# Scores of a gated linear attention on quarters of the TensorE array: 32 keys per matmul with their own queries, collected in a compact tile

## The chip, the cores and the metric

The kernel runs on one core of a Trainium2 chip. Its time is the device time of one execution in microseconds (us), lower is better; of several runs the median is given. Engines are named as in the profile: PE is TensorE (PEld its weight loads), DVE is VectorE, ACT is ScalarE, POOL is GpSimd, SP is SyncE, which issues the transfers.

## The reference, cut to what matters

The reference is one decoder layer over 256 tokens: an RMSNorm, one wide input projection, three branches (gated linear attention, forgetting attention, cross-attention into 256 memory tokens), their gates, an output projection and a final RMSNorm. The change concerns the scores inside the gated linear attention. It has 4 heads with keys of 128 features and a decay for every feature and every token:

```python
b = jnp.cumsum(gi, axis=2)
...
diff = b[:, :, :, None, :] - b[:, :, None, :, :]
decay = jnp.exp(jnp.where(causal[None, None, :, :, None], diff, -jnp.inf))
scores = jnp.einsum('bhid,bhjd,bhijd->bhij', qi, ki, decay)
o_intra = jnp.einsum('bhij,bhje->bhie', scores, vi)
```

The score of query i and key j is a sum over 128 features of q, k and exp(b_i - b_j), with j not after i. All arithmetic is float32.

## The kernel before, in words

**The main work.** Nearly all of the time goes into projections of the normed tokens with float32 weights. Each weight piece of 1024 columns by 128 rows is loaded by SP (tile `raw`), rounded to a high part by ACT (`hi`, line 174) and subtracted to a low part by DVE (`lo`, line 187); PE multiplies with both. `natural` (lines 224 to 226) makes projections with the tokens on partitions, `transposed` (lines 254 and 259) those with the features on partitions. In `transposed` a group of four matmuls of 512 columns (L254) and four of 256 columns (L259) makes one step.

**The order of the work.** The order is written out by hand. Everything that isn't a projection is a Python generator in one of three lanes (`post`, `side`, `main`); after each step of a projection `pull()` advances each lane by one `yield`, and `yield n` leaves n - 1 pulls out. So small work is threaded between projection steps in program order, on each engine's own queue.

**The scores.** `gla_scores` (line 601) runs in the main lane. It treats 8 tiles (4 heads by 2 halves of 128 tokens), each with 128 keys and 128 queries, and a fixed ladder of levels: blocks of 32, of 8, of 2, and single tokens. At a level with blocks of s, the keys are referred to the end of their own block (`E`, lines 687 to 692), and the queries of later blocks inside the same stretch of 4s tokens are referred to the end of the first, second or third block of that stretch (`Q`, 96, 64 and 32 queries of each tile, 192 columns in all, lines 630 to 643). Both factors are exponentials that can't overflow.

For each tile the matmul of L718 multiplies all 128 keys with all 192 prepared queries, 128 partitions by 192 columns. Two tiles share a bank of PSUM, so a level has four groups of two matmuls, one group per pull. Of the 128x192 products only those in which the key's block belongs to the query's reference are wanted. DVE picks them with `copy_predicated` (L732) under a mask from POOL: three instructions per group, one for each part of Q, written into `gA`, the 8 tiles of 128x128 scores. The last level has a matmul with 64 odd queries and all 128 queries, and two instructions per group (masks `gpair` and `ident`). At the end `gla_out` uses `gA` as the weights of L748. A float32 matmul appears as two weight loads and two matmuls in the profile, so the 32 matmuls of L718 are 64 records of each kind.

**The same features elsewhere.** In the forgetting attention, L817 multiplies with 64 weight columns at a time: two heads write the upper and the lower half of one bank's partitions. It is the one place before the change where matmuls use a part of the array's columns.

Of the kernel before, what the change touches and what calls it, by code (L numbers as in the profile page):

```python
# [16 lines left out]
P = 128  # L17
# [34 lines left out]
N_WARM = 7  # L52

STEPS = (32, 8, 2)
Q_OFF = (0, 96, 160)
Q_N = 192
BR_KT = (range(0, 8), range(8, 12), range(12, 16))

# [2 lines left out]
def body(ctx, tc, xw, memT, xn, memn, wall, wsm, wup, cst, fgain, out):  # L61
# [425 lines left out]
        return r  # L487


    gmask = cpool.tile([P, len(STEPS), Q_N], F32, name="gmask")  # L490
    gpair = cpool.tile([P, 64], F32, name="gpair")
    dpool = ctx.enter_context(tc.tile_pool(name="dpool", bufs=1, space=bass.MemoryType.DRAM))
    drow = dpool.tile([1, 8 * S], F32, name="drow")

    def make_masks():

        nc.gpsimd.memset(gmask, 1.0)
        for li, s in enumerate(STEPS):
            for b in range(3):
                w, nb = (3 - b) * s, 32 // s  # L500
                mk_ = gmask[:, li, Q_OFF[b]:Q_OFF[b] + nb * w].rearrange("p (b s) -> p b s", s=w)
                nc.gpsimd.affine_select(out=mk_, in_=mk_, pattern=[[-4 * s, nb], [0, w]],
                                        compare_op=ALU.is_ge, fill=0.0, base=-b * s, channel_multiplier=1)
                nc.gpsimd.affine_select(out=mk_, in_=mk_, pattern=[[4 * s, nb], [0, w]],
                                        compare_op=ALU.is_ge, fill=0.0, base=(b + 1) * s - 1, channel_multiplier=-1)

        nc.gpsimd.affine_select(out=gpair, in_=ones[:, :64], pattern=[[-2, 64]], compare_op=ALU.is_equal,
                                fill=0.0, base=0, channel_multiplier=1)

    def scale_first():  # L510

# [89 lines left out]
    def gla_scores():  # L601
        gB, gq, gk = G["B"], G["q"], G["k"]
        gqf, gkf = gq.rearrange("p h s -> p (h s)"), gk.rearrange("p h s -> p (h s)")
        B4 = gB.rearrange("p (h t i) -> p h t i", h=4, t=2)

        def blocks(x, half, s):

            return x[:, 512 * half:512 * half + 512].rearrange("p (b s) -> p b s", s=s)

        def of_q(Q, b, s):  # L610
            w = (3 - b) * s
            return Q[:, :, Q_OFF[b]:Q_OFF[b] + 32 * (3 - b)].rearrange("p e (b s) -> p e b s", s=w)

        def later(x, half, b, s):

            v = blocks(x, half, 4 * s)[:, :, (b + 1) * s:]
            return v.rearrange("p (e b) s -> p e b s", e=4)

        def prep_keys(s):

            E = a4([P, 1024])
            Bv = gB.rearrange("p (b s) -> p b s", s=s)
            nc.vector.tensor_tensor(out=E.rearrange("p (b s) -> p b s", s=s),
                                    in0=Bv[:, :, s - 1:s].to_broadcast([P, 1024 // s, s]), in1=Bv,
                                    op=ALU.subtract)
            return E

        def prep_queries(s, half):

            Q = a4([P, 4, Q_N])  # L630
            for b in range(3):
                w, nb = (3 - b) * s, 32 // s
                end = blocks(gB, half, 4 * s)[:, :, (b + 1) * s - 1:(b + 1) * s]
                nc.vector.tensor_tensor(
                    out=of_q(Q, b, s), in0=later(gB, half, b, s),
                    in1=end.rearrange("p (e b) s -> p e b s", e=4).to_broadcast([P, 4, nb, w]),
                    op=ALU.subtract)
            return Q

        def times_q(Q, s, half):  # L640
            for b in range(3):
                nc.vector.tensor_tensor(out=of_q(Q, b, s), in0=of_q(Q, b, s),
                                        in1=later(gqf, half, b, s), op=ALU.mult)

        def pick(v, u):
            return v[:, :, u].rearrange("p (e b) -> p e b", e=4)

        def prep_pairs(half):

            Q = a4([P, 4, Q_N])  # L650
            Bh = blocks(gB, half, 2)
            nc.vector.tensor_tensor(out=Q[:, :, :64], in0=pick(Bh, 1), in1=pick(Bh, 0), op=ALU.subtract)
            nc.scalar.copy(Q[:, :, 64:], gqf[:, 512 * half:512 * half + 512].rearrange(
                "p (e i) -> p e i", e=4))
            return Q

        def times_odd(Q, half):
            nc.vector.tensor_tensor(out=Q[:, :, :64], in0=Q[:, :, :64],
                                    in1=pick(blocks(gqf, half, 2), 1), op=ALU.mult)
# [12 lines left out]
        nc.vector.tensor_tensor(out=cd[:, :, 0, :], in0=cd[:, :, 0, :], in1=gk[:, :, :P], op=ALU.mult)  # L672
        nc.vector.tensor_tensor(out=cd[:, :, 1, :], in0=cd[:, :, 1, :], in1=gq[:, :, P:], op=ALU.mult)
        yield 2
        ps = att()
        for h in range(4):
            MM(ps[:, h * P:(h + 1) * P], lhsT=cd[:, h, 0, :], rhs=cd[:, h, 1, :], start=True, stop=True)
        yield 1
        gX = G["X"] = a2([P, 4, P])
        nc.scalar.copy(gX, ps.rearrange("p (a b) -> p a b", a=4))  # L680
        yield from fox_decay()

        for li in range(len(STEPS) + 1):
            s = STEPS[li] if li < len(STEPS) else None
            Qs = []
            if s:
                E = prep_keys(s)
                yield 2
                nc.scalar.activation(E, E, AF.Exp, scale=1.0 / 16)
                Qs.append(prep_queries(s, 0))  # L690
                yield 2
                nc.vector.tensor_tensor(out=E, in0=E, in1=gkf, op=ALU.mult)
                nc.scalar.activation(Qs[0], Qs[0], AF.Exp, scale=1.0 / 16)
                yield 2
                Qs.append(prep_queries(s, 1))
# [5 lines left out]
                yield 2  # L701
            else:
                E = gkf
                for half in range(2):
                    Qs.append(prep_pairs(half))
                yield 2
                for half in range(2):
                    odd = Qs[half][:, :, :64]
                    nc.scalar.activation(odd, odd, AF.Exp, scale=1.0 / 16)
                yield 2  # L710
                for half in range(2):
                    times_odd(Qs[half], half)
                yield 2
            for c in range(4):
                ps = att()[:, :2 * Q_N].rearrange("p (a b) -> p a b", a=2)
                for j in range(2):
                    e = 2 * c + j
                    MM(ps[:, j, :], lhsT=E[:, e * P:(e + 1) * P], rhs=Qs[c // 2][:, e % 4, :],  # L718
                       start=True, stop=True)
                A2 = gA[:, 2 * c:2 * c + 2, :]  # L720
                if s:
                    places = [(A2.rearrange("p a (b s) -> p a b s", s=4 * s)[:, :, :, (b + 1) * s:],
                               gmask[:, li, Q_OFF[b]:Q_OFF[b] + 32 * (3 - b)].rearrange(
                                   "p (b s) -> p b s", s=(3 - b) * s),
                               ps[:, :, Q_OFF[b]:Q_OFF[b] + 32 * (3 - b)].rearrange(
                                   "p a (b s) -> p a b s", s=(3 - b) * s)) for b in range(3)]
                else:
                    places = [(A2.rearrange("p a (b s) -> p a b s", s=2)[:, :, :, 1], gpair, ps[:, :, :64]),
                              (A2, ident, ps[:, :, 64:])]
                yield 1  # L730
                for dst, mask, src in places:
                    nc.vector.copy_predicated(  # L732
                        dst, mask.bitcast(U32).unsqueeze(1).to_broadcast(list(src.shape)), src)
            yield 1

    def gla_out():
        oa = G["o"] = [a4([P, 1024]) for _ in range(NT)]
# [492 lines left out]
```

## Time and profile before

| | before |
|---|---|
| median of 3 runs | 810.05 us (809.97 to 810.63) |
| the profiled execution | 810.0 us |
| its span in the trace | 808.3 us |
| granted PE clock, mean | 0.997 |
| PE records of L718 | 64 loads, 64 matmuls, from 108.8 to 186.3 us |

The profile shows one execution. A group row reads: line, engine, operation, tiles written and read, shape, count, then busy time in us and mean ns of one, then the engine's idle time ahead of them. A row of the timeline reads: start in us, length, engine, line, operation, shape, count. PE's ends are modelled, so what a matmul costs is read from the starts of the rows around it, not from its length.

### The profile page before, as it was taken

To read this page: it belongs to the slowest core of one execution; us is meant where nothing else is said; L and a number is where in the kernel's file an instruction comes from. 1 tells how busy PE (TensorE), PEld (TensorE's weight loads), DVE (VectorE), ACT (ScalarE), POOL (GpSimd) and SP (SyncE) were. 2 spreads that over 40 slices of the span, in tenths; PEclk is the share of its full clock that TensorE was granted. 3 is DMA by queue.
4 is the path that set the end of the run, shared out by engine and by line. 5 is a ranking of instruction groups with operands and counts; after the bars stand their busy time and mean duration, and the time that the engine had idled before them with its cause. 6 is when DMAs were issued, how large, how long until landed. Compare 5 with 4: busy or idle time off the path is not lost.

```text
span 808.3 us, 9931 instructions
## 1 busy us (share of the span) xinstructions
PE 798.4 (99%) x3888; PEld 670.4 (83%) x3888; DVE 495.4 (61%) x697; ACT 403.9 (50%) x558; POOL 18.8 (2%) x36
## 2 busy tenths in 40 slices
PE   9999999999999999999999999999999999999996
PEld 7888888888888788888888888888888888888885
DVE  6767978875656667676445644465446544575653
ACT  6768655644454476565444444434443444444632
POOL 7000000001000000000000000000000000000000
PEclk9999999999999999999999999999999999999998
DMA  9945738455453544445555555555555555548633
GB/s 328 392 186 186 262 135 305 156 205 186 156 207 124 191 144 140 165 177 208 197 177 197 181 191 201 208 178 187 208 175 190 204 176 193 208 162 303 238 129 104
DMA packets 27070, 158.87 MB, mean 197 GB/s; under 512 B 2984, under 2 KB 4528, under 8 KB 10128
## 3 DMA queue, kind: packets, MB, share of 16 engines
q1 hardware_dynamic: 26880, 158.22, 54.7%
q8 instruction: 30, 0.49, 0.2%
q14 instruction: 16, 0.13, 0.0%
q10 hardware_dynamic: 144, 0.02, 0.0%
HBM read 156.13 MB, written 2.11 MB: 196 GB/s over the span
## 4 chain that ended last, share of the span: by engine, by line
PE 95%; DVE 2%; ACT 1%; issue 1%; DMA 0%; SPq 0%; DVEq 0%
PE acc L224 19%; PE acc L226 19%; PE acc L225 19%; PE acc L254 13%; PE acc L259 7%; PE acc L1095 4%; PE acc L1096 4%; PE acc L1094 4%; PE att L254 2%; PE att L718 1%; PE att L259 1%; DVE lo L187 1%; DMA xw<-xw 0%; PE att L443 0%; PE att L1005 0%
## 5 line engine op out<-in xcount | busy, mean ns | idle before, releaser
L187 DVE TENSOR_TENSOR lo<-raw,hi 128x1024 fp32r<-128x1024 f32 x256 | 312.2, 1223 | 198.4 <-ACT hi L174 198.1
L174 ACT CAST hi<-raw 128x1024 fp32r<-128x1024 f32 x256 | 266.4, 1052 | 314.7 <-PE acc L226 239.2
L224 PE MATMUL acc<-hi,x 128*128 128x512 f32 x544 | 214.8, 395 | 0.0
L226 PE MATMUL acc<-hi,x 128*128 128x512 f32 x544 | 212.1, 390 | 0.0
L225 PE MATMUL acc<-lo,x 128*128 128x512 f32 x544 | 212.1, 390 | 0.0
L226 PEld LDWEIGHTS acc<-hi,x 128*128 128x128 f32 x544 | 102.1, 188 | 21.6
L224 PEld LDWEIGHTS acc<-hi,x 128*128 128x128 f32 x544 | 102.2, 188 | 21.1 <-issue 0.8
L225 PEld LDWEIGHTS acc<-lo,x 128*128 128x128 f32 x544 | 102.2, 188 | 20.8 <-DVE lo L187 0.4
L254 PE MATMUL acc<-x,hi 128*128 128x512 f32 x384 | 107.8, 402 | 0.0
L254 PEld LDWEIGHTS acc<-x,hi 128*128 128x128 f32 x384 | 66.8, 189 | 10.3 <-issue 0.8
L259 PEld LDWEIGHTS acc<-x,lo 128*128 128x128 f32 x384 | 58.8, 189 | 8.2
L259 PE MATMUL acc<-x,lo 128*128 128x256 f32 x384 | 61.0, 281 | 0.0
L225 PE MATMUL acc<-lo,oT 128*128 128x512 f32 x128 | 49.8, 389 | 0.0
L226 PE MATMUL acc<-hi,oT 128*128 128x512 f32 x128 | 49.8, 389 | 0.0
L224 PE MATMUL acc<-hi,oT 128*128 128x512 f32 x128 | 49.8, 389 | 0.0
L1094 PE MATMUL acc<-hi,a 128*128 128x512 f32 x96 | 37.5, 391 | 0.0
L1096 PE MATMUL acc<-hi,a 128*128 128x512 f32 x96 | 37.4, 390 | 0.0
L1095 PE MATMUL acc<-lo,a 128*128 128x512 f32 x96 | 37.4, 389 | 0.0
L225 PEld LDWEIGHTS acc<-lo,oT 128*128 128x128 f32 x128 | 24.0, 188 | 5.0
L226 PEld LDWEIGHTS acc<-hi,oT 128*128 128x128 f32 x128 | 24.0, 188 | 5.0
L224 PEld LDWEIGHTS acc<-hi,oT 128*128 128x128 f32 x128 | 24.0, 188 | 5.0
L1096 PEld LDWEIGHTS acc<-hi,a 128*128 128x128 f32 x96 | 18.0, 188 | 3.7
(214 smaller groups left out, 754.4 us busy)
## 6 DMA issues: line engine op xcount, KB each, us to landing
raw<-wall SPq DMA_DIRECT2D x130, 1024.0 KB, 4.7
a<-xn SPq DMA_DIRECT2D x8, 512.0 KB, 7.8
xw<-xw SPq DMA_DIRECT2D x4, 768.0 KB, 6.5
xw<-xw SPq DMA_DIRECT2D x7, 384.0 KB, 5.4
a<-memT SPq DMA_DIRECT2D x4, 512.0 KB, 6.2
a<-memn SPq DMA_DIRECT2D x4, 512.0 KB, 7.5
lraw<-wall SPq DMA_DIRECT2D x2, 1024.0 KB, 6.9
out<-a SPq DMA_DIRECT2D x8, 256.0 KB, 3.2
```

Of the source, the lines that this page charges most:

```text
L174: nc.scalar.copy(hi, raws[q][:, 2 * s:2 * s + 2, :])
L187: nc.vector.tensor_tensor(out=lo, in0=raws[q][:, 2 * s:2 * s + 2, :], in1=parts[n][0].bitcast(F32), op=ALU.subtract)
L224: MM(ps[t], lhsT=h1, rhs=hi, start=(kt == first), stop=False)
L225: MM(ps[t], lhsT=h1, rhs=lo, start=False, stop=False)
L226: MM(ps[t], lhsT=h2, rhs=hi, start=False, stop=(kt == last))
L254: MM(ps[c], lhsT=hi[:, c * P:(c + 1) * P], rhs=h_of(h, kt).rearrange("p a s -> p (a s)"), start=(kt == 0), stop=False, skip_group_check=True)
L259: MM(ps[c][:, :S], lhsT=lo[:, c * P:(c + 1) * P], rhs=h_of(h, kt)[:, 0, :], start=False, stop=(kt == KT - 1), skip_group_check=True)
L718: MM(ps[:, j, :], lhsT=E[:, e * P:(e + 1) * P], rhs=Qs[c // 2][:, e % 4, :], start=True, stop=True)
L1094: MM(ps, lhsT=h1, rhs=hi, start=(kt == 0), stop=False)
L1095: MM(ps, lhsT=h1, rhs=lo, start=False, stop=False)
L1096: MM(ps, lhsT=h2, rhs=hi, start=False, stop=(kt == KT - 1))
```

## The change

The matmul of L718 is cut along the keys. At the levels of 8, of 2 and of single tokens, the columns of Q are laid out so that the 48 queries which belong to each 32 keys stand together; four matmuls, one for each 32 keys, use 32 weight columns and 48 query columns each and write 32 partitions of one bank: 8 tiles by 4 quarters, 32 matmuls per level. At the level of 32, the first three quarters of the keys have 96, 64 and 32 queries, 24 matmuls. All matmuls of a level are issued in one go, and the results of all 8 tiles are picked in the next pull.

The results of the three finer levels are now compact, 8 tiles of 32 columns (`gD`, new, cleared by POOL): three `copy_predicated` per level for all tiles together, two at the last level. At the level of 32 no mask is needed: six plain copies of 32 partitions, four on DVE and two on ACT. At the end four copies (two on DVE, two on ACT) put the four quarters of `gD` on the diagonal blocks of `gA`. The masks are smaller, with a few POOL additions that fold them. The level's pulls are 16 instead of 17, the last level's 9 instead of 11, with 4 pulls after it.

```diff
...
         def of_q(Q, b, s):
-            w = (3 - b) * s
-            return Q[:, :, Q_OFF[b]:Q_OFF[b] + 32 * (3 - b)].rearrange("p e (b s) -> p e b s", s=w)
+
+            w, n = (3 - b) * s, Q_N if s == 32 else Q_N // 4
+            v = Q.rearrange("p e (j c) -> p (e j) c", c=n)
+            lo = sum((3 - i) * n // 6 for i in range(b))
+            return v[:, :, lo:lo + (3 - b) * n // 6].rearrange("p e (b s) -> p e b s", s=w)
...
         gA = G["A"] = a4([P, 8, P])
         nc.gpsimd.memset(gA, 0.0)
+        gD = a2([P, 8, 32])
+        nc.gpsimd.memset(gD, 0.0)
...
-            for c in range(4):
-                ps = att()[:, :2 * Q_N].rearrange("p (a b) -> p a b", a=2)
-                for j in range(2):
-                    e = 2 * c + j
-                    MM(ps[:, j, :], lhsT=E[:, e * P:(e + 1) * P], rhs=Qs[c // 2][:, e % 4, :],
-                       start=True, stop=True)
...
+            if li == 0:
+                pss = [att().rearrange("p (e i) -> p e i", e=4) for _ in range(2)]
+                off, n_q = (0, 96, 160), 3
+            else:
+                ps = att()[:, :8 * 48].rearrange("p (e i) -> p e i", e=8)
+                off, n_q = (0, 48, 96, 144), 4
+            for e in range(8):
+                for j in range(n_q):
+                    n = 96 - 32 * j if li == 0 else 48
+                    dst = pss[e // 4][:, e % 4, P - n:] if li == 0 else ps[:, e, :]
+                    MM(dst[32 * j:32 * j + 32], lhsT=E[:, e * P + 32 * j:e * P + 32 * j + 32],
+                       rhs=Qs[e // 4][:, e % 4, off[j]:off[j] + n], start=True, stop=True,
+                       skip_group_check=True)
...
             yield 1
+            if li == 0:
+                for j in range(3):
+                    q = slice(32 * j, 32 * j + 32)
+                    for c in range(2):
+                        (nc.scalar.copy if j == 1 else nc.vector.tensor_copy)(
+                            gA[q, 4 * c:4 * c + 4, q.stop:], pss[c][q, :, q.stop:])
+            for dst, mask, src in places:
+                nc.vector.copy_predicated(dst, mask.bitcast(U32).to_broadcast(list(src.shape)), src)
+            yield 2
+        for j in range(4):
+            q = slice(32 * j, 32 * j + 32)
+            (nc.scalar.copy if j % 2 else nc.vector.tensor_copy)(gA[q, :, q], gD[q])
+        yield 4
```

PE's queue at the level of 8, before. L718 is the scores' matmul, L254 and L259 are the projection of which the step is part (`acc` its banks, `hi` and `lo` the weights, `x` the tokens):

```order
L259 MATMUL acc_1294<-x_13_145,lo_1308 128x256 x2
L718 MATMUL att_1359<-a_1216,a_1187 128x192 x2
L254 MATMUL acc_1312<-x_13_145,hi_1259 128x512 x2
L254 MATMUL acc_1312<-x_13_145,hi_1261 128x512 x2
L259 MATMUL acc_1312<-x_13_145,lo_1276 128x256 x2
L259 MATMUL acc_1312<-x_13_145,lo_1308 128x256 x2
L718 MATMUL att_1377<-a_1216,a_1187 128x192 x2
L254 MATMUL acc_1263<-x_28_200,hi_1321 128x512 x2
```

The same place with the change (lines are one lower for the projection, and the scores' matmul is L732):

```order
L258 MATMUL acc_1306<-x_13_147,lo_1284 128x256 x2
L258 MATMUL acc_1306<-x_13_147,lo_1316 128x256 x2
L732 MATMUL att_1367<-a_1212,a_1187 32x48 x16
L732 MATMUL att_1367<-a_1266,a_1187 32x48 x16
L253 MATMUL acc_1320<-x_13_147,hi_1271 128x512 x2
L253 MATMUL acc_1320<-x_13_147,hi_1273 128x512 x2
```

Four groups of two matmuls with projection steps between them have become one run of 32 matmuls, one pull later than the first group stood.

DVE's queue at the level of 32, before (L732 here is the masked pick, L187 a low part of weights, L361 a low part of the memory tokens):

```order
L187 TENSOR_TENSOR lo_1098<-raw_964,hi_1086 128x1024
L732 COPY_PREDICATED a_843<-gmask,att_1109 128x2x96
L732 COPY_PREDICATED a_843<-gmask,att_1109 128x2x64
L732 COPY_PREDICATED a_843<-gmask,att_1109 128x2x32
L187 TENSOR_TENSOR lo_1126<-raw_964,hi_1088 128x1024
L361 SCALAR_TENSOR_TENSOR m_136_934<-a_935,cs,m_136_934 128x256
L732 COPY_PREDICATED a_843<-gmask,att_1123 128x2x96
```

The same place with the change:

```order
L186 TENSOR_TENSOR lo_1098<-raw_964,hi_1086 128x1024
L186 TENSOR_TENSOR lo_1143<-raw_964,hi_1088 128x1024
L360 SCALAR_TENSOR_TENSOR m_137_934<-a_935,cs,m_137_934 128x256
L751 COPY a_841<-att_1117 32x4x96
L751 COPY a_841<-att_1118 32x4x96
L751 COPY a_841<-att_1117 32x4x32
L751 COPY a_841<-att_1118 32x4x32
L186 TENSOR_TENSOR lo_1175<-raw_1008,hi_1163 128x1024
```

Twelve masked picks in four portions, with low parts between them, have become four copies in one portion, behind one more low part.

More of the change, by code (lines that the diff above doesn't have):

```diff
@@ L487, in proj_N @@
         return r
-    gmask = cpool.tile([P, len(STEPS), Q_N], F32, name="gmask")
-    gpair = cpool.tile([P, 64], F32, name="gpair")
+    gmask = [cpool.tile([P, 3, 4 * n], F32, name=f"gmask{n}") for n in (1, 4)]
+    gpair = cpool.tile([P, 1, 64], F32, name="gpair")
+    gdiag = cpool.tile([P, 1, P], F32, name="gdiag")
     dpool = ctx.enter_context(tc.tile_pool(name="dpool", bufs=1, space=bass.MemoryType.DRAM))
@@ L707, in gla_scores @@
                 for half in range(2):
[L708 to L709 removed]
+                    nc.scalar.activation(odd(Qs[half]), odd(Qs[half]), AF.Exp, scale=1.0 / 16)
                 yield 2
```

71 lines of the change are left out of this document (34 added, 37 removed).

## The prediction

> **What bounds the kernel now.** I read the page first: busy time and the chain that ended last.
>
> ```profile
> span 808.3 us, 9931 instructions
> PE 798.4 (99%) x3888; PEld 670.4 (83%) x3888; DVE 495.4 (61%) x697; ACT 403.9 (50%) x558; POOL 18.8 (2%) x36
> PE 95%; DVE 2%; ACT 1%; issue 1%; DMA 0%; SPq 0%; DVEq 0%
> ```
>
> PE is busy throughout and carries 95% of the chain, so the question is what the change does to PE's time. The execution of this profile took 810.0 us, its span is 808.3 us and 1.7 us lie around it; the median of the runs is 810.05 us, so I sum against 810.0. A difference of 0.2%, 1.6 us, is about the least that a measurement of this kernel can tell from no change.
>
> Next the waits between 95 and 225 us, the stretch with the scores.
>
> ```profile
> DVE a L732 <- PE att L718: 11.4, 9, 2.5
> DVE lo L187 <- ACT hi L174: 8.2, 7, 1.8
> PEld att L781 <- issue: 0.4, 1, 0.4
> ```
>
> DVE waits for PE (the masked picks, 11.4 us). PE has 0.7 us of waiting in the answer, of which the longest is shown. Nothing that DVE or ACT is spared can shorten this stretch; only PE's own work counts.
>
> What a group of L718 costs is read from the starts of PE's rows, first with a group in each step, then without.
>
> ```profile
> 108.92 0.81 PE L718 MATMUL att<-a,a 128*128 128x192 f32 x4
> 109.44 1.22 PE L254 MATMUL acc<-x,hi 128*128 128x512 f32 x4
> 110.50 0.63 PE L259 MATMUL acc<-x,lo 128*128 128x256 f32 x4
> 110.97 0.81 PE L718 MATMUL att<-a,a 128*128 128x192 f32 x4
> 113.53 0.76 PE L254 MATMUL acc<-x,hi 128*128 128x512 f32 x2
> ...
> 117.11 1.09 PE L254 MATMUL acc<-x,hi 128*128 128x512 f32 x4
> 119.92 1.09 PE L254 MATMUL acc<-x,hi 128*128 128x512 f32 x4
> ```
>
> From 109.44 to 113.53 lie two steps with a group, 2.045 us each; from 117.11 to 119.92 two without, 1.405 us each. A group costs 0.64 us, 0.16 us for each of its four records of 192 columns. So 48 columns should stream in 0.04 us. The 16 groups cost 10.2 us. That is all the change can win, and only if its own matmuls cost less.
>
> **The change part by part.** *Streaming on quarters of the array.* One place shows matmuls on part of the columns, L817 with 64.
>
> ```profile
> 239.52 0.64 PE L259 MATMUL acc<-x,lo 128*128 128x256 f32 x4
> 240.09 0.87 PE L817 MATMUL att<-b,a 128*64 128x256 f32 x8
> 241.92 0.64 PE L259 MATMUL acc<-x,lo 128*128 128x256 f32 x4
> ...
> 240.09 0.44 PE L817 MATMUL att<-b,a 128*64 128x256 f32 x2
> ...
> L817 PEld LDWEIGHTS att<-b,a x32: 132/137/138, 240.1 to 276.8; 128*64 128x64 f32 x32
> L718 PEld LDWEIGHTS att<-a,a x64: 187/190/193, 108.8 to 186.1; 128*128 128x128 f32 x64
> ```
>
> The last timeline row was asked for a window of 0.02 us: two of its matmuls start in it, one for each half of the columns. The whole step takes 241.92 - 239.52 = 2.40 us where one without a group takes 1.405, so the eight records cost 1.00 us. At 0.16 us per 192 columns, each half's four records (two of 256 columns, two of 128) stream for 0.64 us, both halves in turn for 1.28. So the halves do run side by side, and 0.36 us is the price of changing the array over and back: PE empties ahead of the group and after it, and the weights ahead of the next matmul can't be loaded early. 64 weight columns fewer take 0.053 us less to load (190 against 137 ns), so a first load of 32 columns is 0.03 us shorter than this one: 0.33 us per run. With four runs that is 1.3 us. If quarters run side by side as halves do, a level streams for 8 tiles x 2 x 0.04 = 0.64 us, the level of 32 (its first quarter has 96 queries) for 1.28 us. No row of the trace has four parts at once.
>
> *Records.* What grows is their number: a matmul on a quarter needs its own load and, being float32, is two loads and two matmuls. A level had 8 matmuls, 32 records; it gets 32 matmuls, 128 records, and the level of 32 gets 96. How fast PE is fed with records, the trace shows only where PE had nothing queued, and how many can be queued, where its sequencer passes a mark.
>
> ```profile
> 7.17 0.30 PEld L254 LDWEIGHTS att<-x,hi 128*128 128x128 f32 x2 [0.80 <-ACT hi L130]
> 7.20 0.47 PE L254 MATMUL att<-x,hi 128*128 128x512 f32 x1 [0.63 <-DVE x L361]
> ...
> L1005 PEldq EVENT_SEMAPHORE  x2: 51/51/51, 628.5 to 716.5; - x2
> 632.35 0.37 PEld L1005 LDWEIGHTS att<-ident,a 128*128 128x128 f32 x2
> 628.51:632.34 3.83, 3.83 (x18) 3.17 (x17) 1.60 (x2) 1.99 (x2) 0.00 (x0) 1.00 0.46 150
> ...
> 788.20:794.20 6.00, 6.00 (x52) 6.00 (x51) 3.71 (x12) 1.74 (x4) 0.00 (x0) 1.00 0.17 62
> ```
>
> At 7.17 PE had been waiting and its queue was empty; the matmul of that load starts 0.03 us after it. At 240.09 two matmuls out of a filled queue started within 0.01 us. The semaphore instruction at 628.5 stands ahead of the transposes of L1005, whose first load starts at 632.35; in between lie 18 matmuls and 17 loads, one of each under way at the start, so the sequencer runs about 33 records ahead. And between 788.2 and 794.2 it supplies about 103 records in 6.0 us, 0.06 us each, which is no more than PE takes there. So a record costs the sequencer between 0.007 us (a filled queue, which isn't its rate) and 0.06. I take 0.028 us: the row at 7.17, at the lower side of its rounding, since it may hold some latency of the matmul.
>
> *The sum.* PE starts a level with some 33 records queued and eats them faster than they are replaced; then it goes at the sequencer's pace. Level of 32: 0.33 + 63 x 0.028 = 2.1 us. Each other level: 0.33 + 95 x 0.028 = 3.0 us, three of them 9.0. Together 11.1 us against 10.2: 0.8 us longer with the unrounded terms. In formula 1.3 + 348 r against 10.2, with r the price of a record; they meet at r = 0.026.
>
> *A rule that speaks against such a cut.* The trace has no matmul under 128 columns. The Trainium skill, "TensorEngine Tiling (Array Packing)", Instruction Overhead, says that each matmul has about 60 cycles of overhead on trn2, that one of a single column takes as long as one of 60, and that no tiling should be taken from a dimension that is small already; 48 is. By "TensorE: Matmul & The Clock Gate", Wait — 56ns, not 53.3ns?, starts never come closer than about 25 ns; with one such interval for each of the 240 matmul records the groups would cost 6.0 + 1.3 = 7.3 us, an estimate, and the kernel would gain 2.9. The two starts at 240.09, 0.01 us apart, speak against such an interval between parts of the array.
>
> *Picks.* DVE loses these:
>
> ```profile
> L732 DVE COPY_PREDICATED a<-gmask,att 128x192 f32<-128x192 uint32 x12 | 4.8, 398 | 6.7 <-PE att L718 6.7
> L732 DVE COPY_PREDICATED a<-gmask,att 128x128 f32<-128x128 uint32 x12 | 3.6, 300 | 0.4
> L732 DVE COPY_PREDICATED a<-gmask,att 128x64 f32<-128x64 uint32 x12 | 3.0, 253 | 0.4
> L732 DVE COPY_PREDICATED a<-ident,att 128x256 f32<-128x256 uint32 x4 | 1.8, 449 | 0.1
> L732 DVE COPY_PREDICATED a<-gpair,att 128x128 f32<-128x128 uint32 x4 | 1.8, 448 | 4.7 <-PE att L718 4.7
> L750 DVE COPY a<-att 128x512 f32<-128x512 f32 x3 | 2.1, 692 | 3.4 <-PE att L748 3.4
> ```
>
> Together 15.0 us. It gets two levels with one of each of the first three forms (1.9 us), one of each of the next two (0.9), and six copies of 128 to 384 columns, each under the 0.69 us of 512: at most 4.2. DVE saves 8 us or more and ACT gains four copies, under 3 us. Neither is on PE's path here (PE waits for them 0.0 to 0.7 us), so the gain is nothing, between zero and 0.7. What DVE's wait holds up is a low part of the weights, the last row of the piece of its queue shown above: it stands behind four copies (under 2.8 us), and PE needs it after five and a half more steps of 1.405 us, 7.7 us after the level's matmuls. It stays covered; uncovered, it would cost what the copies last. POOL's masks are made early and its 18.8 us lie beside everything; SP's queue keeps its order. The finer levels' matmuls wait for both halves of Q, one pull later than their first group did, so nothing arrives later for them.
>
> **The rivals.**
>
> *Fed fast enough.* If a record costs 0.02 us or less, the quarters show: at 0.02 the groups cost 1.6 + 3 x 2.2 = 8.3 us (gain 2.0, 808.0), at 0.007 the streaming decides and they cost 4.6 (gain 5.6, 804.4). For it: the halves at 240.09 really overlap, and a row at 7.17 may be latency rather than rate. Against it: that row is the only one with an empty queue, and says 0.03. The page's interval of 25 ns would fall inside this case.
>
> *The sequencer becomes the bound and is slower.* Place: records 34 to 128 of every level. The steady stretch from 788.2 allows up to 0.06 us. At 0.04 the groups cost 15.2 us (815.0), at 0.06 22.2 us (822). It decides from 0.030 on, where the loss passes 1.6 us. For it: nothing in the trace shows a faster steady supply. Against it: the matmul at 7.20.
>
> *The quarters don't run side by side.* The change then doesn't do what it says. Every tile streams 8 records of 0.04 us in turn, 2.6 us per level, 2.9 with the changeover, 11.6 us in all: 1.3 us slower, 811.3. L817 speaks against it for halves; for quarters nothing does.
>
> **How the numbers follow.** My forecast, a supply of 0.022 to 0.034 us per record, gives 808.7 to 812.9; I give it 0.46, of which 0.34 lie within 1.6 us of 810 and 0.12 above. Fed fast enough: 0.33, all faster. Slower sequencer: 0.14. Quarters in turn: 0.07, within the bound. So faster 0.33, same 0.41, slower 0.26. The time is that of r = 0.028, 810.8 us. The range reaches from the end of the fast case, 804.4, to the upper end of the forecast, 813.0, and leaves out the slow sequencer and little else, some 0.15. Both signs lie in it; the forecast's own range is 808.7 to 812.9.
>
> **What would show it.** In the profile after, the scores' matmuls (lines 732 to 734) stand in four runs. Right: a level of 48 columns takes about 3 us of PE from the end of the projection's step to its next, its first 16 or so matmul records start in bundles of four and the rest in pairs of load and matmul some 0.06 us apart. Wrong towards faster: bundles of four to the end and a level under 1.5 us. Wrong towards slower: pairs further apart than 0.07 us. Also wrong: a wait of PE for DVE or ACT between 95 and 190 us, or DVE busy no less than 8 us under its 495.

## The result and the profile after

The changed kernel takes 804.19 us (803.53 to 805.48, 6 runs), the kernel before 810.01 us (809.72 to 810.63, 6 runs): ratio 0.9927, 95% interval 0.9917 to 0.9938. It is faster by 0.7%, where 810.8 was forecast. The time lies 0.2 us below the range and next to what the rival "fed fast enough" gave, 804.4.

First the page of the changed kernel: span, instructions, busy time.

```profile
span 801.8 us, 10259 instructions
PE 792.7 (99%) x4064; PEld 663.5 (83%) x4064; DVE 486.7 (61%) x667; ACT 406.5 (51%) x562; POOL 15.3 (2%) x33
PE 95%; DVE 2%; ACT 1%; issue 1%; DMA 0%; SPq 0%; DVEq 0%
```

PE has 176 matmul records more (240 against 64) and is busy 5.7 us less; it still carries 95% of the chain. DVE is busy 8.7 us less and ACT 2.6 us more.

Next PE's timeline of the changed kernel around the level of 32 and around the first finer level. The columns are start and duration in us, engine, line, operation, partitions x columns, elements, number. One line below the change has moved: L253 and L258 are the projection's matmuls that stood at L254 and L259, and L732 are the scores.

```profile
109.60 0.64 PE L258 MATMUL acc<-x,lo 128*128 128x256 f32 x4
110.17 1.51 PE L732 MATMUL att<-a,a 128*32 128x96 f32 x48
111.60 1.21 PE L253 MATMUL acc<-x,hi 128*128 128x512 f32 x4
112.65 0.64 PE L258 MATMUL acc<-x,lo 128*128 128x256 f32 x4
...
133.69 0.64 PE L258 MATMUL acc<-x,lo 128*128 128x256 f32 x4
134.25 0.89 PE L732 MATMUL att<-a,a 128*32 128x48 f32 x64
135.07 1.21 PE L253 MATMUL acc<-x,hi 128*128 128x512 f32 x4
136.12 0.40 PE L258 MATMUL acc<-x,lo 128*128 128x256 f32 x2
```

From L258 to the next L258 lie 3.05 us with the level of 32 and 2.43 with a finer one; a step without scores takes 1.405. So the level of 32 costs 1.64 us and a finer level 1.02. The two others are alike (0.89 us for 64 records), so the scores cost 1.64 + 3 x 1.02 = 4.7 us, where the 16 groups of before cost 10.2: 5.5 us. Nearly the same is seen when the 3,568 records of the projections are put side by side, one by one. The changed kernel is 0.25 us ahead at 103 us and 5.94 us ahead from 405 us to the last of these records, so 5.69 us come from the stretch between. What differs between executions lies ahead of it: the profiles of all the changed kernels stand between 0.25 us ahead and 0.98 us behind at 103 us.

Something else lies behind it. From the start of PE's last matmul to the end the profiled execution of the kernel before takes 8.29 us and that of the changed kernel 7.76. The last output transfer is issued at the same place in both, by 4.11 us after that start; SP goes on at 7.17 us in one and at 6.46 in the other. So some 0.5 us of the difference between these two executions isn't the scores, and why the output lands sooner stays open. In the kernels below this stretch is 8.46 us ("order of one run"), 8.45 us ("halves of the array") or 7.56 to 7.76 us (all others), so their times and gains differ by tenths.

Now the first records of that finer level, in narrowing windows of the same timeline: each row counts the records that overlap its window.

```profile
134.25 0.25 PE L732 MATMUL att<-a,a 128*32 128x48 f32 x4
...
134.25 0.29 PE L732 MATMUL att<-a,a 128*32 128x48 f32 x8
...
134.25 0.34 PE L732 MATMUL att<-a,a 128*32 128x48 f32 x12
...
134.70 0.44 PE L732 MATMUL att<-a,a 128*32 128x48 f32 x24
```

The windows end at 134.28, 134.345 and 134.39; the last runs from 134.90 to 134.94. Four records start together, and in the starts of the trace, which are finer than these rows, it goes on so to the sixteenth four: the four quarters 6.7 ns apart, each step 0.0425 us after the one ahead (0.067 after the first). The last record starts 0.68 us after the first. This is the sign that the prediction named for the faster side: bundles of four to the end and a level under 1.5 us.

Last, what L732 is, and who waits for it.

```profile
L732 PEld LDWEIGHTS att<-a,a x240: 106/110/113, 110.2 to 171.9; 128*32 128x32 f32 x120
L732 PEldq EVENT_SEMAPHORE  x2: 51/51/51, 134.4 to 157.6; - x2
  DVE b L754: 6.0, 2
  DVE a L751: 2.1, 1
```

128 records, loads and matmuls, go through in 0.68 us, 0.0053 us each. Even a semaphore instruction of 51 ns in their midst (134.4) leaves the steps of 0.0425 as they are. Between 95 and 225 us DVE waits for PE, as before, and PE never for DVE or ACT.

### The profile page after: what moved, and what is told of

Same layout as the page of the kernel before. It is cut to its first block, busy times and chain, and to the rows that moved or that the text cites. A ratio compares the mean times of both kernels' runs of the same rounds, so it can differ in the third digit from the quotient of the medians.

```text
span 801.8 us, 10259 instructions
## 1 busy us (share of the span) xinstructions
PE 792.7 (99%) x4064; PEld 663.5 (83%) x4064; DVE 486.7 (61%) x667; ACT 406.5 (51%) x562; POOL 15.3 (2%) x33
## 4 chain that ended last, share of the span: by engine, by line
PE 95%; DVE 2%; ACT 1%; issue 1%; DMA 0%; SPq 0%; DVEq 0%
PE acc L223 19%; PE acc L225 19%; PE acc L224 19%; PE acc L253 13%; PE acc L258 7%; PE acc L1120 4%; PE acc L1119 4%; PE acc L1121 4%; PE att L253 2%; PE att L258 1%; DVE lo L186 1%; PE att L732 0%; PE att L442 0%; DMA xw<-xw 0%; PE att L1030 0%
## 5 line engine op out<-in xcount | busy, mean ns | idle before, releaser
L186 DVE TENSOR_TENSOR lo<-raw,hi 128x1024 fp32r<-128x1024 f32 x256 | 312.0, 1222 | 204.6 <-ACT hi L173 204.4
L253 PE MATMUL acc<-x,hi 128*128 128x512 f32 x384 | 107.1, 400 | 0.0
L253 PEld LDWEIGHTS acc<-x,hi 128*128 128x128 f32 x384 | 66.3, 189 | 10.7 <-issue 1.0
L258 PEld LDWEIGHTS acc<-x,lo 128*128 128x128 f32 x384 | 58.8, 189 | 8.2
L258 PE MATMUL acc<-x,lo 128*128 128x256 f32 x384 | 61.0, 280 | 0.0
```

The source lines that it names most:

```text
L186: nc.vector.tensor_tensor(out=lo, in0=raws[q][:, 2 * s:2 * s + 2, :], in1=parts[n][0].bitcast(F32), op=ALU.subtract)
L253: MM(ps[c], lhsT=hi[:, c * P:(c + 1) * P], rhs=h_of(h, kt).rearrange("p a s -> p (a s)"), start=(kt == 0), stop=False, skip_group_check=True)
L258: MM(ps[c][:, :S], lhsT=lo[:, c * P:(c + 1) * P], rhs=h_of(h, kt)[:, 0, :], start=False, stop=(kt == KT - 1), skip_group_check=True)
```

## Experiments

Every kernel below computes the whole reference. The kernel before ran beside them at medians of 810.1, 810.3 and 809.9 us. The gain in the last column is read as above: by how much PE moves ahead of the kernel before from 103 us on, by the records of the projections. It leaves out what differs ahead of that and behind PE's last matmul, comes from one profiled execution of each kernel, and was 5.69 in both profiles of the changed kernel.

| kernel | us, median (range, runs) | ratio to before, interval | gain, us |
|---|---|---|---|
| before, order of one run | 810.37 (809.91–810.92, 10) | 1.0003 [0.9994, 1.0012] | -0.1 |
| quarter by quarter | 809.6 (809.21–811.3, 10) | 0.9991 [0.9982, 1.0001] | 0.0 |
| four runs a level | 807.73 (807.51–809.37, 8) | 0.9972 [0.9961, 0.9982] | 1.77 |
| picks four times | 803.9 (803.72–804.17, 4) | 0.9922 [0.9907, 0.9937] | 5.6 |
| half the columns | 805.59 (805.39–806.04, 4) | 0.9940 [0.9923, 0.9957] | 4.0 |
| a short extra matmul | 807.07 (806.11–808.07, 4) | 0.9957 [0.9942, 0.9971] | 3.1 |
| halves around quarters | 805.21 (805.03–805.61, 5) | 0.9942 [0.9929, 0.9956] | 4.43 |
| halves of the array | 808.16 (807.97–809.23, 7) | 0.9974 [0.9963, 0.9985] | 2.03 |
| balanced and merged | 804.09 (803.91–804.57, 4) | 0.9921 [0.9906, 0.9935] | 5.27 |
| balanced alone | 804.10 (803.70–804.28, 5) | 0.9926 [0.9913, 0.9938] | 5.81 |
| balanced, merged, pulls kept | 803.58 (803.35–804.09, 5) | 0.9921 [0.9909, 0.9934] | 6.16 |
| changed kernel again | 804.19 (804.05–804.78, 5) | 0.9929 [0.9917, 0.9941] | 5.69 |

**The order alone.** The kernel before, with a level's eight full matmuls issued in one go. Is it the quarters that win, or only that the groups stand together?

```diff
+            banks = []
             for c in range(4):
                 ps = att()[:, :2 * Q_N].rearrange("p (a b) -> p a b", a=2)
+                banks.append(ps)
                 for j in range(2):
                     e = 2 * c + j
                     MM(ps[:, j, :], lhsT=E[:, e * P:(e + 1) * P], rhs=Qs[c // 2][:, e % 4, :],
                        start=True, stop=True)
+            for c in range(4):
+                ps = banks[c]
                 A2 = gA[:, 2 * c:2 * c + 2, :]
```

> The kernel before, with the eight full matmuls of a level issued in one go and its picks left as they were, one group per pull. Side by side (the gain comes from quarters of the array that stream at the same time, and is paid for with one changeover per run): no quarters, no gain; each matmul still streams 192 columns, the level costs PE about 2.6 us, and the time stays at 810.0, within 0.5 us. Order (the gain comes from one run per level in place of four groups): most of the 5.8 us, so 804 to 806.

The timeline of this kernel at its level of 32:

```profile
108.63 0.63 PE L259 MATMUL acc<-x,lo 128*128 128x256 f32 x4
109.10 2.76 PE L720 MATMUL att<-a,a 128*128 128x192 f32 x16
111.56 1.23 PE L254 MATMUL acc<-x,hi 128*128 128x512 f32 x4
112.63 0.63 PE L259 MATMUL acc<-x,lo 128*128 128x256 f32 x4
```

From L259 to the next L259 lie 4.00 us, 2.60 more than a step without scores: sixteen records of 192 columns in one run cost about what four groups apart cost, 2.56. Ratio 1.0003: standing together is worth nothing by itself, the gain comes from the quarters.

**Quarter by quarter.** The same 240 records with the two loops exchanged, so that one quarter's eight matmuls come ahead of the next quarter's.

```diff
-            for e in range(8):
-                for j in range(n_q):
+            for j in range(n_q):
+                for e in range(8):
```

> The changed kernel with its two loops exchanged: first the first quarter of all 8 tiles, then the second, and so on. Same matmuls, same picks, same output. Side by side: quarters can overlap only if PE reaches past the records of one quarter (32 at the finer levels, of about 33 that are queued ahead). If it starts them in their order, a finer level streams 64 x 0.042 = 2.7 us plus 0.33 for the changeover, 3.0 instead of 1.0, and the level of 32 about 2.9 instead of 1.6: 7.3 us more than the change, 811.5. If it reaches past them, less. Order, or DVE's relief: nothing changes, 804.2.

The timeline of this kernel at the first finer level, then two windows of it, to 135.21 and from 135.20 to 135.60:

```profile
134.63 0.64 PE L258 MATMUL acc<-x,lo 128*128 128x256 f32 x4
135.19 2.49 PE L732 MATMUL att<-a,a 128*32 128x48 f32 x64
137.61 0.97 PE L253 MATMUL acc<-x,hi 128*128 128x512 f32 x3
...
135.19 0.23 PE L732 MATMUL att<-a,a 128*32 128x48 f32 x1
...
135.19 0.57 PE L732 MATMUL att<-a,a 128*32 128x48 f32 x9
```

One record starts where four did, and nine in 0.4 us where the changed kernel starts some 37 (four per 0.0425). The level takes 2.42 us to the next L253 instead of 0.82 and the whole gain of the scores is gone (0.0 in the table; the time, 809.6, is a little under before's, which fits the 7.75 us behind the last matmul here). In the starts, a quarter's records are 0.0425 us apart, and the next quarter's first starts when three of this quarter's sixteen have yet to start. So PE seems to look past about three waiting matmuls and no further; the quarters overlap at the seams only. (The trace doesn't name a record's quarter; it is read from two series of starts, each 0.0425 us apart, that interleave for three steps.) That is why the loss was 5.7 us by the gains and not the 7.3 of quarters strictly in turn. Same instructions, same number, same loads: only their order decides whether quarters run side by side.

**Four runs a level.** Twelve changeovers of the array more: two tiles, then a pull of the projection, and so on; of the three pulls added to a level two are taken away around it (one at the last level).

```diff
-                yield 3
+                yield 2
...
+                if e % 2 and e < 7:
+                    yield 1
...
-            yield 2
+            yield 1
```

> The changed kernel with each level's matmuls cut into four runs of two tiles, one per pull, with projection steps between them; picks as in the change. Side by side: the streaming stays, but there are 16 changeovers instead of 4; at 0.33 us each that is 4.0 us more, 808.2. If the changeover costs PE nothing beyond the streaming: 804.2. Order: 810.

The timeline of this kernel, two runs of the level of 32:

```profile
108.97 0.52 PE L732 MATMUL att<-a,a 128*32 128x96 f32 x12
109.42 1.19 PE L253 MATMUL acc<-x,hi 128*128 128x512 f32 x4
110.45 0.63 PE L258 MATMUL acc<-x,lo 128*128 128x256 f32 x4
111.01 0.52 PE L732 MATMUL att<-a,a 128*32 128x96 f32 x12
```

It takes 3.5 us more than the changed kernel by the medians, 3.9 by the gains: 0.30 to 0.33 us for each further changeover. The price read from L817 (0.33) holds.

**The picks four times.** DVE gets 24 picks more, and so its busy time of before back.

```diff
-            for dst, mask, src in places:
+            for dst, mask, src in 4 * places:
```

> The changed kernel with every masked pick done four times over (the output is the same), so that DVE gets back about 8.4 us of busy time between 110 and 180 us. Side by side: PE doesn't wait for DVE there, 804.2 within 0.5 us, and DVE's busy time near 495 us. DVE's relief (part of the gain comes from the picks that DVE lost): it goes back towards 810, at least 2 us of it.

The page of this kernel:

```profile
PE 793.1 (99%) x4064; PEld 663.8 (83%) x4064; DVE 495.8 (62%) x691; ACT 406.4 (51%) x562; POOL 15.6 (2%) x33
```

DVE is busy 495.8 us, as before, and the time is 803.9 (0.9922): DVE's relief is worth nothing.

**The price of a record.** In the changed kernel the streaming (0.0425 us for a step of four) hides what a record costs. Three kernels shorten the streaming of a record, so that the price shows. First every matmul as two of half the columns: 256 records in a finer level instead of 128, the same columns in all.

```diff
-                    MM(dst[32 * j:32 * j + 32], lhsT=E[:, e * P + 32 * j:e * P + 32 * j + 32],
-                       rhs=Qs[e // 4][:, e % 4, off[j]:off[j] + n], start=True, stop=True,
...
+                    for a in (0, n // 2):
+                        MM(dst[32 * j:32 * j + 32, a:a + n // 2],
+                           lhsT=E[:, e * P + 32 * j:e * P + 32 * j + 32],
+                           rhs=Qs[e // 4][:, e % 4, off[j] + a:off[j] + a + n // 2], start=True, stop=True,
...
```

> The changed kernel with each quarter matmul cut into two of half the columns (24 at the finer levels), each with its own weight load: 256 records per finer level instead of 128, the same columns streamed, the same output. Free records (what PE is fed with costs nothing at this rate): the start distance inside a quarter halves to 0.021 us, the time stays at 804.2. Load bound (a matmul can't start before its 32 weight columns are in, about 0.027 us by half of the 0.053 us that 64 columns took): distance 0.03, a finer level streams 32 x 0.03 = 0.96 instead of 0.68 us, 805.0. Feed bound at the 0.0053 us per record that the changed kernel reached: 223 x 0.0053 = 1.18 us per finer level, 805.7; at a slower feed of 0.028 us, 6 us per level, over 820.

Its timeline at the first finer level:

```profile
134.53 1.45 PE L733 MATMUL att<-a,a 128*32 128x24 f32 x128
135.91 0.96 PE L253 MATMUL acc<-x,hi 128*128 128x512 f32 x3
```

1.38 us to the next L253 instead of 0.82; to the last start 1.263 us, 0.0099 for a load with its matmul. The kernel takes 805.59 us, near the 805.7 of the feed bound. A further matmul of 8 columns ahead of each, overwritten by it:

```diff
+                    for w in (8, n):
+                        MM(dst[32 * j:32 * j + 32, :w], lhsT=E[:, e * P + 32 * j:e * P + 32 * j + 32],
+                           rhs=Qs[e // 4][:, e % 4, off[j]:off[j] + w], start=True, stop=True,
...
```

> The changed kernel with one more matmul of 8 columns ahead of each quarter matmul, on the same weights and overwritten by it: twice the records, hardly more columns, the same output. Free records: 8 columns stream in 0.007 us, 16 more steps of it per finer level, 0.1 us, 804.7. Load bound: each extra step takes 0.027 to 0.03 us, 0.45 us per level, four levels 1.8 us, 806.0. Feed bound at 0.0053 us per record: a finer level 1.18 us against 0.68, and 0.15 for the level of 32 (which is under its streaming), 805.7. The trace tells load from feed: under the load bound the steps alternate between 0.03 and 0.042 us, under the feed bound they are even.

```profile
134.82 1.59 PE L733 MATMUL att<-a,a 128*32 128x8 f32 x128
136.34 0.96 PE L253 MATMUL acc<-x,hi 128*128 128x512 f32 x3
```

This timeline of it shows 1.52 us; 0.0108 us for a load with its matmul, and 807.07 us, more than any theory gave (the level of 32 takes 0.5 us more as well). In the trace its starts lie 0 to 46 ns apart, neither even nor in turns of 0.03 and 0.042 us, so the sign that was to tell load from feed decides nothing. Neither tells a price of records from a price of the order: in both kernels four records of one quarter stand in a row, and PE looks past about three. So the halves go around the quarters, and two stand in a row as in the changed kernel:

```diff
             for e in range(8):
-                for j in range(n_q):
...
+                for half in range(2):
+                    for j in range(n_q):
+                        n = 96 - 32 * j if li == 0 else 48
+                        a = half * (n // 2)
...
+                        MM(dst[32 * j:32 * j + 32, a:a + n // 2],
...
```

> As the run with half columns (256 records in a finer level), but the halves lie around the quarters: two matmul records of a quarter stand in a row instead of four. If PE looks past only about three waiting matmuls, that run was slow because of its order, and here a step of four takes some 0.021 to 0.03 us: a finer level 0.7 to 0.95 us instead of 1.35, the kernel at 804.2 to 804.9. If a pair of load and matmul has a price of its own (0.0099 us each there, 0.0108 with the short extra matmuls), the order changes nothing: 1.27 us to the last start of a level, the kernel at 805.6.

Its timeline at the first finer level:

```profile
134.07 0.64 PE L258 MATMUL acc<-x,lo 128*128 128x256 f32 x4
134.64 1.28 PE L734 MATMUL att<-a,a 128*32 128x24 f32 x128
135.85 0.96 PE L253 MATMUL acc<-x,hi 128*128 128x512 f32 x3
```

1.21 us: between the two theories, and 805.21 lies between 804.9 and 805.6. Both are at work. The order accounts for 0.17 us a level (1.38 to 1.21). The rest is a price. In the starts, some 36 records go in steps of four, 0.0317 us apart where 24 columns need 0.021. From there on they go two by two, 0.0165 us from pair to pair, to the last at 135.73. The bundles change there and the pace hardly: a load with its matmul takes 0.0079 us at first and 0.0083 then, 0.0042 for each record. Whether the sequencer's supply, the loads or a start sets this isn't told apart; as a price of supply it is an upper bound.

**Halves of the array instead.** The finer levels with 64 keys on half the columns and 96 queries: half the records, twice the streaming, and 24 short picks a level on DVE (16 at the last).

```diff
-                off, n_q = (0, 48, 96, 144), 4
+                parts = [(64 * h, 64, 96 * h, 96, 0) for h in range(2)]
...
-                for j in range(n_q):
+                for k, w, o, n, d in parts:
+                    MM(pss[e // 4][k:k + w, e % 4, d:d + n], lhsT=E[:, e * P + k:e * P + k + w],
+                       rhs=Qs[e // 4][:, e % 4, o:o + n], start=True, stop=True,
...
```

> The changed kernel with halves of the array at the finer levels: 64 keys and 96 queries per matmul, 16 matmuls per level, picked quarter by quarter (24 short picks per level, so DVE has more to do); the level of 32 as in the change. Side by side: each finer level streams 8 x 2 x 0.08 = 1.28 instead of 0.68 us, three levels 1.8 us more, 806.0. If the gain came from anything but the number of parts (fewer queries per key, compact results): 804.2.

The timeline of this kernel's PE, then of DVE's picks of one level, then of the weight loads; the bracket is the idle time ahead and what ended it:

```profile
135.11 1.54 PE L729 MATMUL att<-a,a 128*64 128x96 f32 x32
136.59 1.21 PE L253 MATMUL acc<-x,hi 128*128 128x512 f32 x4
...
136.11 5.69 DVE L755 COPY_PREDICATED b<-gmask,att 32x96 f32<-32x96 uint32 x24 [2.07 <-PE att L729]
...
145.38 0.30 PEld L258 LDWEIGHTS acc<-x,lo 128*128 128x128 f32 x2 [0.55 <-DVE lo L186]
169.06 0.19 PEld L224 LDWEIGHTS acc<-lo,x 128*128 128x128 f32 x1 [0.57 <-DVE lo L186]
183.35 0.30 PEld L258 LDWEIGHTS acc<-m,lo 128*128 128x128 f32 x2 [0.53 <-DVE lo L186]
```

1.47 us to L253 in the starts instead of 0.82: 0.65 us in each of three levels, 2.0 us, near the 1.8 expected. But the kernel took 808.16 and not 806.0. Once after each finer level PE waits for the low part of a weight, L186, which stood behind the picks on DVE: 0.55 + 0.57 + 0.53 = 1.65 us. Together 3.6 us, the difference of the gains (5.69 against 2.03); the rest of the 4.0 us between the medians may lie in the stretch behind the last matmul, 8.45 us here. It is a cover such as the prediction named at the level of 32, here at the finer levels: uncovered, the wait costs PE, though less than the picks last. In the run "picks four times" the picks of these levels last 4.0, 4.5 and 3.8 us, and PE doesn't wait; here they last 5.7, 6.0 and 4.9.

**A better version?** The level of 32 is bound by its quarter with 96 queries. Balanced over four quarters (64, 64, 32 and 32 columns), and the last two levels in one run, which saves a changeover:

```diff
-                off, n_q = (0, 96, 160), 3
+                parts32 = ((0, 0, 64, 32), (1, 96, 64, 64), (2, 160, 32, 96), (3, 64, 32, 0))
...
+            elif li == 2:
+                kept = (E, Qs)
+                continue
...
+                runs = [(s, E, Qs)] if li == 1 else [(2,) + kept, (s, E, Qs)]
```

> A version meant to be faster than both: at the level of 32 the first quarter's 96 queries are divided, 64 on their own quarter and 32 on the fourth quarter, which was idle there; and the matmuls of the last two levels stand in one run. Side by side with a price per changeover: the level of 32 streams 8 x 2 x 0.053 = 0.85 instead of 1.3 us, and one changeover less saves 0.3 us: 0.75 us faster than the change, 803.4. If PE's stretch is no longer what counts there, or the later picks hold up the last step: 804.2 or more.

804.09 us, not to be told from the changed kernel: the records are ahead of the changed kernel's by 0.4 us at 233 us, and the gain ends at 5.27. The edit left out three pulls of the projection where the skipped level had been, so everything behind stood elsewhere. The loss has one place, a weight load of the cross-attention in this kernel's timeline:

```profile
326.99 0.73 PEld L899 LDWEIGHTS att<-b,a 128*128 128x128 f32 x4 [0.84 <-DVE b L912]
```

PE waits 0.84 us for a copy on DVE; the changed kernel has no such wait there. The two parts were then separated. Balance alone, with every pull in its place:

```diff
-                off, n_q = (0, 96, 160), 3
+                parts = ((0, 0, 64, 32), (1, 96, 64, 64), (2, 160, 32, 96), (3, 64, 32, 0))
...
+                    k = 32 * (j % 3) if li == 0 else 32 * j
```

> The changed kernel with only the level of 32 balanced over four quarters of the array (64, 64, 32 and 32 columns instead of 96, 64 and 32); every pull where it was. The level's run took 0.87 us instead of 1.26 in the kernel that also merged two levels. If that gain stays in the end time, this is 0.4 us under the changed kernel run beside it; if what lies behind gives it back, as that kernel's trace suggests, there is no difference.

The timeline of this kernel, of PE, then of DVE and ACT behind the level, then of the weight loads:

```profile
110.91 1.09 PE L732 MATMUL att<-a,a 128*32 128x64 f32 x64
111.93 1.21 PE L253 MATMUL acc<-x,hi 128*128 128x512 f32 x4
...
111.70 0.41 DVE L752 COPY a<-att 32x256 f32<-32x256 f32 x1 [1.94 <-PE att L732]
114.03 0.26 ACT L752 COPY a<-att 32x128 f32<-32x128 f32 x1 [0.35 <-DVE a L752]
114.19 1.99 ACT L173 CAST hi<-raw 128x1024 fp32r<-128x1024 f32 x2
115.27 1.23 DVE L186 TENSOR_TENSOR lo<-raw,hi 128x1024 fp32r<-128x1024 f32 x1 [1.27 <-ACT hi L173]
127.21 0.42 DVE L243 TENSOR_TENSOR a<-acc,a 128x256 f32<-128x256 f32 x1
...
127.74 0.75 PEld L253 LDWEIGHTS acc<-x,hi 128*128 128x128 f32 x4 [0.32 <-issue]
```

The level takes 1.02 us to L253 instead of 1.43, and PE is 0.42 us further ahead by 127 us. Then 0.36 of it is lost at one place: the load at 127.74 comes after 0.32 us of idle time, which the changed kernel doesn't have there. The profile names no releaser, but the semaphore that PE's sequencer waits for just ahead of this load is updated at 127.64, as DVE ends L243, which empties a bank of the projection. The eight copies alternate between DVE and ACT on one tile and hand over to each other each time. Counted from the level's first matmul, ACT's next cast of a weight starts at 3.28 us instead of the changed kernel's 2.54; DVE's low part behind it is late by the same 0.74 us, DVE has no idle time from there on, and L243 comes 0.59 us late. That the copies are the cause is argued from these rows, not tried. 0.12 us of gain is left, and 804.10 can't be told from 804.19. And both parts with the three pulls put back:

```diff
                 kept = (E, Qs)
+                yield 3
                 continue
```

> Balanced level of 32 and the last two levels in one run, as in the kernel that gave its gain back, but with three pulls of the stream put in where the skipped level had them, so that the work behind stays where it was. If the moved pulls gave the gain back: 0.4 us for the balance and 0.3 us for one changeover less, 0.7 us under the changed kernel run beside it. If not: no difference to it.

```profile
170.97 0.39 PE L225 MATMUL acc<-hi,x 128*128 128x512 f32 x1
171.29 1.57 PE L744 MATMUL att<-a,a 128*32 128x48 f32 x128
172.79 0.50 PE L253 MATMUL acc<-m,hi 128*128 128x512 f32 x1
```

The timeline of this kernel at its merged run: 128 matmul records in 1.50 us to L253, where two runs of 0.82 would be 1.64, and what PE loses ahead of a run is paid once. The gain is 6.16 us, 0.35 more than balance alone, the price of one changeover, and 0.89 more than without the three pulls: the wait for DVE at 326.99 isn't there, so moving the pulls had given the gain back. It takes 803.58 us (803.35 to 804.09). Beside it ran

> The changed kernel itself, beside the three others on the same chip: 804.2 us.

which took 804.19 (804.05 to 804.78). Only one of the five runs, 804.09, is not below all of these, and 0.47 of the 0.6 us between the medians is seen in the traces (6.16 against 5.69). But the intervals of the two ratios overlap, and by its ratio, 0.9921, it stands level with "picks four times" (0.9922) and "balanced and merged" (0.9921). So its gain on PE is the largest here; that it is the fastest kernel isn't shown by the times.

## Why the prediction was wrong

The step that failed is the price of a record, "I take 0.028 us: the row at 7.17". The row showed a load and the matmul that it feeds, out of an empty queue: the time from one to the other, and by the runs not the pace of a supply. The prediction named that doubt ("it may hold some latency of the matmul") and took the row all the same, because it was the only one with an empty queue. The runs put the price at 0.0053 us or less where streaming hides it, and at no more than 0.0042 with the halves around the quarters. What a finer level costs instead, in the prediction's own terms, is 0.33 for the changeover and 0.68 for streaming: 1.01 us, where the sum had 3.0; measured 1.02. The level of 32 is 0.33 and 1.28, 1.61 us, where the sum had 2.1; measured 1.64.

The second half of the same step fell too: "it goes at the sequencer's pace" after some 33 records. Nothing changes in the changed kernel after 33 records, nor at a semaphore. A lead of 33 records was a reading of how far ahead the sequencer was. It says nothing on how fast it can go when PE takes records faster. Only with the halves around the quarters do the bundles change midway, after some 36 matmuls, 72 records with their loads, and the pace by 4%; whether a queue runs out there stays open.

The lower bound of that price, 0.007, was too high as well, though it did little harm: two starts 0.01 us apart were taken for the fastest that could be, and at 0.007 supply and streaming are level (95 x 0.007 = 0.67 against 0.64; 4.6 us, 804.4). That end of the range had no margin for how far runs of one kernel lie apart (803.53 to 805.48), nor for what lies behind the last matmul, and the median fell 0.2 us outside. That the time came so near to 804.4 is in part luck: the sum holds nothing of that last stretch.

What the Trainium skill says was weighed lightly, and that held. The Trainium skill, "TensorE: Matmul & The Clock Gate", Wait — 56ns, not 53.3ns?, says that starts don't come closer than about 25 ns; here four quarters start 6.7 ns apart. Within one quarter the steps that can be told apart are 31.7 ns or more, so for a single quarter no run here speaks against it. The Trainium skill, "TensorEngine Tiling (Array Packing)", Instruction Overhead, advises against taking a tiling factor from a dimension that is small already. The change takes its factor from the 128 keys, which aren't few, and leaves 48 columns; in each of four quarters these stream at the full rate, 0.0425 us against 0.16 for 192. With 24 columns a step took 0.0317 us instead of 0.021: there something of a fixed price begins to show.

What held, point by point:

- The groups of L718 cost 10.2 us, and that is what could be won: 4.7 are paid now.
- Streaming, 0.04 us for 48 columns: 0.0425.
- Quarters run side by side, as halves did. But only in this order; the prediction took the order for granted.
- The changeover, 0.33 us: 0.30 to 0.33 by the twelve further ones, 0.35 by the one that was saved.
- DVE saves "8 us or more": 8.7, and it is worth nothing (picks four times, 0.9922).
- The low part of a weight behind the copies stays covered in the changed kernel. At the finer levels, behind 24 short picks, it doesn't, and costs 1.65 us.
- The order of the groups by itself: nothing (1.0003).

## What to carry to other kernels

Price an instruction stream by a stretch in which many short ones follow each other, not by one start out of an empty queue, and if there is no such stretch, give the case without that price the larger chance when other rows (the two halves side by side) already show it at work. Matmuls on parts of the array gain only if neighbours in program order lie on different parts; put the loop over the parts inside. After a gain on the busiest engine, look at what stands behind the place on the other engines: moved pulls took back 0.89 us and, as far as the rows tell, handed-over copies 0.36, as much as a good step had won.

## What the runs showed of the hardware

- Four column quarters of the array take float32 matmuls side by side, starts 6.7 ns apart. The loads of 32 weight columns (110 ns each) are hidden as well.
- PE reaches about three waiting matmuls ahead, as read from the starts. With a quarter's sixteen in a row the same 64 records take 2.42 us instead of 0.82 to the next projection matmul.
- 128 records, loads and matmuls, went through in 0.68 us. With 24 columns, where streaming is too short to hide it, a load with its matmul took about 0.0083 us.
- A run of matmuls on parts of the array costs 0.30 to 0.35 us for changing over and back, in runs of 12 to 128 records.
